# A differential-attention layer on Trainium2: context scores computed between the two maps' latent scores, with one bias operation per map

## The chip, the core and the metric

The kernel runs on one core of a Trainium2 chip. The metric is the device time of one execution in microseconds (us); a lower time is better. The core has a matrix engine (TensorE, PE in the profile; its weight loads are listed apart as PEld), a vector engine (VectorE, DVE), a scalar engine (ScalarE, ACT), GpSimd (POOL) and SyncE (SP), which issues DMAs here. Each engine runs its own queue of instructions in order, and waits on semaphores for the others.

## The reference

Four transformer layers over 1024 latent and 256 context tokens, width 1024. Layers 0 and 3 use grouped attention, layer 1 a windowed attention, layer 2 the differential attention that this change is about:

```
def diff_attention(q, k, v, lam):
    def block(j, qb):
        logits = jnp.einsum("bqhmd,bkhmd->bhmqk", qb, k).astype(jnp.float32) * scale
        p = jax.nn.softmax(logits, axis=-1)
        a = (p[:, :, 0] - lam * p[:, :, 1]).astype(v.dtype)
        return jnp.einsum("bhqk,bkhd->bqhd", a, v)
...
o = finish(diff_attention(q, jnp.concatenate([kc, k], axis=1),
                          jnp.concatenate([vc, v], axis=1), lam), s)
```

A head has two maps, m = 0 and 1, each with a softmax of its own over 256 context keys and 1024 latent keys. The second map is subtracted with the factor lam. The softmax needs the largest logit of a row, as a bias of the exponential: bias = -scale * max(largest context logit, largest latent logit).

## The kernel before

The differential layer first projects all tokens (`run_blocks`), and then attends (`project_attend`, `tile_events`, `head_c`). There are 8 heads. A head is cut into 8 tiles of 128 queries, followed by one tile for the context queries. The parts of a tile are functions: `near` (context scores of both maps and their maxima), `scores0` and `scores1` (latent scores of a map, their maximum, and the bias), `exps0` and `exps1` (the exponentials), `sums` (the factor of the second map and the combination), `turn0`, `turn_near` and `turn1` (transposes of the combined map), `products` (times v), and, every four tiles, `gate`, `scale` and `finish`.

`tile_events` gives tile number t the time t + offset for each part, with the offsets of a small table in `layer_c`, sorts all the parts by that time, and emits them so. Each of the four compute engines then keeps that order. So parts of several tiles interleave: while tile t does its scores, `sums` and `turn0` belong to tiles before it, and `turn_near`, `turn1` and `products` to the tile three before it. Loads of the next head are emitted 7 tiles ahead.

In the order before, a tile starts on TensorE with `near` (L1454: four products of 256 columns, tile `sc`), then `scores0` (L1464 by way of L1398 and L1399: four of 512 columns, tile `st`), the transposes of `turn_near` and `turn1` (tile `pT`), `scores1`, `turn0`, and `products` (tile `o`). VectorE has, for the same tile, L1456 (maximum of `sc`, two columns: one for each map), L1457 (times -scale, in place, both columns), L1466 (maximum of `st`, one column), L1467 (times -scale and the smaller of it and column m of `mx`), then L1466 and L1467 again for the second map. ScalarE's first exponential (L1478 for the context, L1482 for the latent keys) reads column m of `mx`. GpSimd combines the maps after L1405 of `sums`: L1412 and L1413 on the context part (`pc`), then on the upper half of the latent part (`p`); VectorE does the lower half in L1492.

PSUM has two tag groups: `pa`, two buffers of 1024 columns (the `st` tiles), and `pb`, four buffers of 512 columns (`sc`, all `pT`, `o`). A tile of a group takes the buffer that was released longest ago, and its first product waits until the last reader of that buffer is done.

Of the kernel before, what the change touches and what calls it, by code (L numbers as in the profile page):

```python
# [15 lines left out]
ALU = mybir.AluOpType  # L16
# [4 lines left out]
P = 128  # L21
# [51 lines left out]
class Net:  # L73
# [1285 lines left out]
    def head_c(self, q, k, i0, vsrc, gain, og, pair, need_ctx):  # L1359


        nc = self.nc
        SC = HD**-0.5
# [27 lines left out]
        def group(g, nq):  # L1391
            st["s", g] = self.small([P, 4, 2], "cs", 6)
            st["ss", g] = self.small([P, 16], "ss", 6)[:, :nq]
            st["o", g] = self.slot([P, 4, P], name="ol")[:, :nq]

        def product(ps, q_, key, m, sl):
            k1, k2 = st[key, m][1:]
            nc.tensor.matmul(ps, q_, k1[:, sl], start=True, stop=False)  # L1398
            nc.tensor.matmul(ps, q_[0 : HD + 1], k2[0 : HD + 1, sl], start=False, stop=True)  # L1399
# [43 lines left out]
        def tile(j):  # L1443
            t = self.Tile()
            g, i = j // 4, j % 4
            d = {}

            def near():

                if i == 0:  # L1450
                    group(g, 4)
                pc = d["pc"] = self.pb("sc").rearrange("p (m k) -> p m k", m=2)
                for m in range(2):
                    product(pc[:, m, :], st["lat", m][0][:, j * P : (j + 1) * P], "ctx", m, slice(0, CTX))  # L1454
                mx = d["mx"] = self.small([P, 2], "mx", 4)
                nc.vector.tensor_reduce(out=mx, in_=pc, axis=AX.X, op=ALU.max)  # L1456
                nc.vector.tensor_scalar_mul(mx, mx, -SC)  # L1457

            def scores(m):
                mx = d["mx"]  # L1460
                ps = d["ps", m] = self.pa("st")
                for c in range(2):
                    sl = slice(c * 512, c * 512 + 512)
                    product(ps[:, sl], st["lat", m][0][:, j * P : (j + 1) * P], "lat", m, sl)  # L1464
                ml = self.small([P, 1], "ml", 4)
                nc.vector.tensor_reduce(out=ml, in_=ps, axis=AX.X, op=ALU.max)  # L1466
                nc.vector.scalar_tensor_tensor(  # L1467
                    out=mx[:, m : m + 1], in0=ml, scalar=-SC, in1=mx[:, m : m + 1], op0=ALU.mult, op1=ALU.min
                )

            def exps(m):
                mx, pc = d["mx"], d["pc"]
                if m == 0:
                    d["s"] = self.small([P, 2, 2], "sm", 4)
                    both = self.slot([P, 3, CTX], name="pc")
                    d["xc"], d["tc"] = both[:, :2], both[:, 2]
                s = d["s"]
                nc.scalar.activation(  # L1478
                    d["xc"][:, m, :], pc[:, m, :], AF.Exp, scale=SC, bias=mx[:, m : m + 1], accum_out=s[:, m, 0:1]
                )  # L1480
                x = d["x", m] = self.slot([P, SEQ], name="p")
                nc.scalar.activation(  # L1482
                    x, d["ps", m], AF.Exp, scale=SC, bias=mx[:, m : m + 1], accum_out=s[:, m, 1:2]
                )

            def sums():
                s, xc = d["s"], d["xc"]
                x0, x1 = d["x", 0], d["x", 1]
                S = st["s", g][:, i : i + 1, :]
                nc.vector.tensor_tensor(S[:, 0], s[:, :, 0], s[:, :, 1], op=ALU.add)  # L1490
                r = ratio(S)
                nc.vector.scalar_tensor_tensor(  # L1492
                    out=x0[:, :512], in0=x1[:, :512], scalar=r, in1=x0[:, :512], op0=ALU.mult, op1=ALU.add
                )
                combine(xc[:, 0, :], xc[:, 1, :], r)
                combine(x0[:, 512:], x1[:, 512:], r)

            def turn(h):
                if h == 0:
                    d["t"] = self.slot([P, SEQ], name="pt")  # L1500
                pt = self.pb("pT")
                for b in range(4):
                    sl = slice((h * 4 + b) * P, (h * 4 + b + 1) * P)
                    nc.tensor.transpose(pt[:, b * P : (b + 1) * P], d["x", 0][:, sl], self.ident)
                half = d["t"][:, h * 512 : h * 512 + 512]
                if h:
                    nc.scalar.activation(half, pt, AF.Copy)
                else:
                    nc.vector.tensor_copy(half, pt)

            def turn_near():
                pt = self.pb("pT")
                for b in range(2):
                    sl = slice(b * P, (b + 1) * P)
                    nc.tensor.transpose(pt[:, sl], d["xc"][:, 0, sl], self.ident)
                nc.scalar.activation(d["tc"], pt[:, :CTX], AF.Copy)

            def products():
                cut = lambda a, b: a[:, b * P : (b + 1) * P]
                value(g, i, [(cut(d["tc"], b), 8 + b) for b in range(2)] + [(cut(d["t"], b), b) for b in range(8)])  # L1520

            if i == 3:
                last(t, g, 4)
            t.near, t.sums, t.products, t.turn_near = near, sums, products, turn_near
            t.scores0, t.scores1 = lambda: scores(0), lambda: scores(1)
            t.exps0, t.exps1 = lambda: exps(0), lambda: exps(1)
            t.turn0, t.turn1 = lambda: turn(0), lambda: turn(1)
            return t
# [47 lines left out]
    def layer_c(self, l, j, need_ctx, extra):  # L1576
        ins, nc = self.ins, self.nc
        w = ins["c_w_in"][j]
        init = 0.8 - 0.6 * math.exp(-0.3 * l)
        pairs = 5 if need_ctx else 4  # L1580
        sg = self.small([P, 1], "subg", 1)
        g = ins["c_subln_g"]
        self.queue(lambda: self.dma(sg, bass.AP(tensor=g.tensor, offset=g.offset + j * P, ap=[[1, P], [1, 1]])))
        self.in_order(lambda: nc.vector.tensor_scalar_mul(sg, sg, 1.0 - init), self.order)

        kscr = [self.Heads(self, "k", swap=True) for _ in range(2)]
        qscr = [self.Heads(self, "q") for _ in range(2)]
        vscr = [self.dram([TOK, 512], name="v") for _ in range(2)]
        ktab = self.rope_tables(ins["c_k_g"][j : j + 1])
        qtab = self.rope_tables(ins["c_q_g"][j : j + 1])  # L1590
        whole = lambda f, n: self.pair_steps([(slice(0, 512), f)], n)
        blocks = [(1024 + b * 512, whole(self.proj_qk(kscr[b], *ktab), 5)) for b in range(2)]
        blocks += [(b * 512, whole(self.proj_qk(qscr[b], *qtab), pairs)) for b in range(2)]
        blocks += [(2048 + b * 512, whole(self.proj_rows(vscr[b]), 5)) for b in range(2)]
        groups = range(3 if need_ctx else 2)
        blocks += [(3072 + b * 512, self.z_steps(4 * b, groups)) for b in range(2)]
        self.in_order(lambda: setattr(self, "lam", self.lambdas(j, init)), self.order)
        og = self.og
        vc, heads = {}, []

        def vget(b):
            if b not in vc:
                vc[b] = []
                for t0, n in GROUPS:
                    s = self.slot([P, n, 256], name="vl")
                    cs = slice(b % 2 * 256, b % 2 * 256 + 256)
                    self.dma(s, vscr[b // 2][t0 * P : (t0 + n) * P, cs].rearrange("(t p) c -> p t c", p=P))
                    vc[b].append(s)
            return vc[b]

        for b in range(4):
            for pr in range(2):

                def vsrc(b=b, pr=pr):
                    vt = vget(b)
                    return lambda kt: vt[kt // 4][:, kt % 4, pr * P : (pr + 1) * P]

                heads.append(
                    self.head_c(
                        qscr[b // 2], kscr[b // 2], b % 2 * 4 + 2 * pr, vsrc, sg, og, 2 * b + pr, need_ctx  # L1620
                    )
                )
        offsets = dict(
            near=0, scores0=0.01, scores1=0.13, exps0=0.21, exps1=0.22, sums=1.58, turn0=2.6, turn_near=3.04,
            turn1=3.08, products=3.82, gate=4.09, scale=5.77, finish=6.75,
        )
        self.project_attend(w, blocks, self.tile_events(heads, offsets, extra), 0)
        return og
# [105 lines left out]
```

## Time and profile before

| what | value |
|---|---|
| median of 3 runs | 3613.51 us (3613.27 to 3614.67) |
| the profiled execution's own time | 3609.91 us |
| its span, first to last instruction | 3608.1 us |
| PE busy | 3471.8 us (96% of the span) |
| DVE busy | 2057.5 us (57%) |
| POOL busy | 1915.1 us (53%) |
| ACT busy | 1320.9 us (37%) |
| DMA, mean share of 16 engines | 34.5% |

Shares over the whole span average over four different layers. The attention of the differential layer is the stretch from about 2267 to 2704 us, 437 us or 12% of the span. A busy PE is not PE at its peak, since matmuls overlap and their ends are modelled. "Idle before" is time in which an engine had nothing running, with the instruction that released it. A row of an instruction gives its duration from start to end; on VectorE the next instruction can start a little before the one ahead has ended.

### The profile page before, as it was taken

The page shows a single profiled execution, that of the slowest core. Times are in us where ns is not written, and L with a number is a line of the kernel's source. Part 1 is how long each engine was busy: PE and PEld are TensorE (multiplying, and loading weights), DVE is VectorE, ACT ScalarE, POOL GpSimd, SP SyncE. Part 2 cuts the span into 40 slices and gives each one's busy share as a digit, 9 for nine tenths or more (in the row PEclk, how much of TensorE's full clock was granted, in tenths as well). Part 3 has the DMA queues.
Part 4 walks back from the last instruction along what each step waited for, and adds up shares of the span by engine and source line. Part 5 has one row for each costly group of instructions (what it writes and reads, how often), then busy time and mean ns, then how long its engine had stood idle before and what let it go on. Part 6 is the DMA issues. An engine that isn't in the chain of part 4 may idle for free.

```text
span 3608.1 us, 49956 instructions
## 1 busy us (share of the span) xinstructions
PE 3471.8 (96%) x18594; PEld 2608.3 (72%) x18594; DVE 2057.5 (57%) x3358; ACT 1320.9 (37%) x2756; POOL 1915.1 (53%) x1854
## 2 busy tenths in 40 slices
PE   7999999998999999999999999999999999999989
PEld 4887444446788888887878888888887787554447
DVE  5552555665641412888566610799994654466653
ACT  3221444451321212774222211677771322344430
POOL 5540666677531311667565510566775643377884
PEclk9999999999999999999999999999999999999999
DMA  6343443513344434552425531221312335111113
GB/s 211 78 122 101 140 138 113 192 56 97 122 105 129 111 123 113 169 153 69 146 79 140 136 114 56 84 82 44 96 42 95 120 79 142 47 40 44 45 41 88
DMA packets 229453, 370.33 MB, mean 103 GB/s; under 512 B 34088, under 2 KB 124120, under 8 KB 229212
## 3 DMA queue, kind: packets, MB, share of 16 engines
q1 hardware_dynamic: 228636, 367.01, 34.5%
q8 instruction: 147, 2.41, 0.3%
q14 instruction: 94, 0.77, 0.1%
q10 hardware_dynamic: 576, 0.15, 0.0%
HBM read 270.36 MB, written 96.57 MB: 102 GB/s over the span
## 4 chain that ended last, share of the span: by engine, by line
PE 73%; DVE 14%; POOL 7%; issue 3%; ACT 1%; DMA 1%; SPq 0%; POOLq 0%; ACTq 0%; DVEq 0%
PE proj L382 22%; PE zT L467 11%; PE y L911 9%; PE o L739 7%; PE st L714 4%; PE st L715 4%; DVE ml L1466 3%; PE sl L670 2%; PE o L1136 2%; POOL p L753 2%; DVE wlo L133 1%; PE qkT L437 1%; POOL rstd L146 1%; PE ada L195 1%; PE pT L1214 1%
## 5 line engine op out<-in xcount | busy, mean ns | idle before, releaser
L753 POOL TENSOR_TENSOR p<-p,p 128x1024 f32<-128x1024 f32 x224 | 540.1, 2411 | 303.6 <-PE o L739 258.2
L382 PE MATMUL proj<-whi,hhi 128*128 128x512 f32 x1408 | 556.3, 395 | 3.7 <-POOL whi L130 2.4
L382 PE MATMUL proj<-wlo,hhi 128*128 128x512 f32 x1408 | 550.8, 391 | 3.0 <-DVE wlo L133 3.0
L382 PE MATMUL proj<-whi,hlo 128*128 128x512 f32 x1408 | 550.4, 391 | 0.0
L719 ACT ACTIVATE p<-st 128x1024 f32<-128x1024 f32 (+1 forms) x336 | 324.1, 1003 | 286.2 <-PE st L715 274.3
L911 PE MATMUL y<-whi,ogt 128*128 128x512 f32 x1216 | 387.5, 396 | 13.2 <-POOL ogt L130 9.4
L661 DVE TENSOR_REDUCE M<-sl 128x1 f32<-128x512 f32 (+1 forms) x326 | 209.8, 685 | 293.2 <-PE sl L670 243.5
L133 DVE TENSOR_TENSOR wlo<-wraw,whi 128x1024 fp32r<-128x1024 f32 x136 | 217.3, 1612 | 221.6 <-POOL whi L130 196.3
L739 PE MATMUL o<-p,v 128*64 128x512 f32 x1344 | 321.2, 599 | 0.0
L130 POOL TENSOR_SCALAR whi<-wraw 128x1024 fp32r<-128x1024 f32 x136 | 178.7, 1319 | 252.6 <-DMA wraw<-in_c_w_in_dram 86.0
L382 PEld LDWEIGHTS proj<-whi,hhi 128*128 128x128 f32 x1408 | 265.7, 189 | 57.9 <-POOL whi L130 2.6
L382 PEld LDWEIGHTS proj<-wlo,hhi 128*128 128x128 f32 x1408 | 265.6, 189 | 57.6 <-DVE wlo L133 4.7
L382 PEld LDWEIGHTS proj<-whi,hlo 128*128 128x128 f32 x1408 | 265.3, 188 | 55.2
L911 PEld LDWEIGHTS y<-whi,ogt 128*128 128x128 f32 x1216 | 229.8, 189 | 67.8 <-POOL ogt L130 11.6
L467 PE MATMUL zT<-hhi,whi 128*128 128x512 f32 (+1 forms) x704 | 256.9, 365 | 5.6 <-DVE qklo L133 5.6
L404 ACT ACTIVATE y<-proj 128x1024 f32<-128x1024 f32 (+1 forms) x68 | 65.6, 964 | 527.0 <-PE proj L382 469.4
L467 PE MATMUL zT<-hhi,wlo 128*128 128x512 f32 (+1 forms) x704 | 254.5, 362 | 1.3 <-DVE wlo L133 1.3
L467 PE MATMUL zT<-hlo,whi 128*128 128x512 f32 (+1 forms) x704 | 254.5, 362 | 0.0
L911 PE MATMUL y<-wlo,ogt 128*128 128x512 f32 x608 | 238.6, 392 | 0.0
L146 POOL TENSOR_TENSOR rstd<-rstd,mhalf 128x16 f32<-128x16 f32 (+3 forms) x132 | 231.0, 1750 | 10.9
L714 PE MATMUL st<-q,k 128*128 128x512 f32 x512 | 217.8, 425 | 10.5 <-DVE M L658 7.2
L658 DVE TENSOR_REDUCE M<-sl 128x2 f32<-128x1024 f32 (+1 forms) x165 | 200.6, 1216 | 45.2 <-PE sl L670 40.1
(221 smaller groups left out, 7035.2 us busy)
## 6 DMA issues: line engine op xcount, KB each, us to landing
adaw<-in_ada_w_dram SPq DMA_DIRECT2D x96, 512.0 KB
xo<-xres SPq DMA_DIRECT2D x86, 256.0 KB
wraw<-in_a_w_in_dram SPq DMA_DIRECT2D x40, 512.0 KB
k<-k SPq DMA_DIRECT2D x40, 512.0 KB
q<-qkhi SPq DMA_DIRECT2D x76, 256.0 KB
q<-qklo SPq DMA_DIRECT2D x76, 256.0 KB
q<-q SPq DMA_DIRECT2D x136, 128.0 KB
wraw<-in_b_w_in_dram SPq DMA_DIRECT2D x32, 512.0 KB
```

Of the source, the lines that this page charges most:

```text
L130: self.nc.gpsimd.tensor_scalar(out=out, in0=in_, scalar1=1.0, scalar2=0.0, op0=ALU.mult, op1=ALU.add)
L133: self.nc.vector.tensor_tensor(out, a, b, op=ALU.subtract)
L146: nc.gpsimd.tensor_tensor(r, r, self.mhalf[:, :n], op=ALU.pow)
L382: nc.tensor.matmul(ps[:, i, :], self.h_op(a, 2 * tp + i, k), wop(b, k), start=(k == 0 and j == 0), stop=(k == KT - 1 and j == 2),)
L467: nc.tensor.matmul(ps, wop(a, k)[:, b * P : (b + 1) * P], self.h_cols(c, g, k), start=(k == 0 and j == 0), stop=(k == KT - 1 and j == 2),)
L658: nc.vector.tensor_reduce(out=out, in_=both.rearrange("p (h q k) -> p h q k", h=2, q=n), axis=AX.X, op=ALU.max)
L661: nc.vector.tensor_reduce(out=out[:, hh, :], in_=ps[hh].rearrange("p (q k) -> p q k", q=n), axis=AX.X, op=ALU.max)
L714: nc.tensor.matmul(ps[:, hh, :], self.k_op(K, 0, kt), q1[:, hh, :], start=True, stop=False)
L719: nc.scalar.activation(p, ps, AF.Exp, scale=HD**-0.5)
L739: nc.tensor.matmul(st["o"][hh * HD : (hh + 1) * HD, :], v(hh, kt), p[:, hh, :], start=j == 0, stop=j == N - 1, tile_position=(0, hh * HD),)
L753: eng.tensor_tensor(a, a, p, op=ALU.add)
L911: nc.tensor.matmul(ps, ot[a][:, k, :], wop[h](b, k), start=(k == 0 and j == 0), stop=(k == KT - 1 and j == 2))
```

## The change

The score of map 0 over the latent keys now comes first, the context scores second (between `turn_near` and `turn1` of the tile three before), and the score of map 1 third, where it was. The scaling of both context maxima (L1457) is gone. In its place a map's bias is made by one operation: the larger of its two maxima, times -scale. It is a `tensor_scalar` that takes the latent maximum as its tensor and the context maximum as a per-partition scalar read from SBUF; before it was a `scalar_tensor_tensor` with two tensors.

```
+            def bias(m):
+                mx = d["mx"][:, m : m + 1]
+                nc.vector.tensor_scalar(out=mx, in0=d["ml", m], scalar1=mx, scalar2=-SC, op0=ALU.max, op1=ALU.mult)
...
                 nc.vector.tensor_reduce(out=mx, in_=pc, axis=AX.X, op=ALU.max)
-                nc.vector.tensor_scalar_mul(mx, mx, -SC)
+                bias(0)
...
-                ml = self.small([P, 1], "ml", 4)
+                ml = d["ml", m] = self.small([P, 1], "ml", 4)
                 nc.vector.tensor_reduce(out=ml, in_=ps, axis=AX.X, op=ALU.max)
-                nc.vector.scalar_tensor_tensor(
-                    out=mx[:, m : m + 1], in0=ml, scalar=-SC, in1=mx[:, m : m + 1], op0=ALU.mult, op1=ALU.min
-                )
+                if m:
+                    bias(m)
...
-            near=0, scores0=0.01, scores1=0.13, exps0=0.21, exps1=0.22, sums=1.58, turn0=2.6, turn_near=3.04,
+            scores0=0, near=0.07, scores1=0.13, exps0=0.21, exps1=0.22, sums=1.58, turn0=2.6, turn_near=3.04,
```

On VectorE, in one tile in the middle of the first head, these rows stood between two L1492 before (`sc`, `st` and `pT` are PSUM tiles, `mx` and `ml` the maxima):

```order
L1492 SCALAR_TENSOR_TENSOR p_19207<-p_19210,rs_19285,p_19207 128x512
L1509 COPY pt_19293<-pT_19294 128x512
L1421 COPY ol_18951<-o_19300 128x128
L1456 TENSOR_REDUCE mx_19319<-sc_19314 128x2
L1457 TENSOR_SCALAR mx_19319<-mx_19319 128x2
L1466 TENSOR_REDUCE ml_19327<-st_19322 128x1
L1467 SCALAR_TENSOR_TENSOR mx_19319<-ml_19327,mx_19319 128x1
L1466 TENSOR_REDUCE ml_19345<-st_19340 128x1
L1467 SCALAR_TENSOR_TENSOR mx_19319<-ml_19345,mx_19319 128x1
```

The same tile in the changed kernel (its line numbers are 1 to 3 higher; L1450 is the new operation, L1469 the latent maximum, L1460 the context maximum):

```order
L1494 SCALAR_TENSOR_TENSOR p_19202<-p_19205,rs_19279,p_19202 128x512
L1511 COPY pt_19287<-pT_19288 128x512
L1421 COPY ol_18958<-o_19294 128x128
L1469 TENSOR_REDUCE ml_19313<-st_19308 128x1
L1460 TENSOR_REDUCE mx_19324<-sc_19319 128x2
L1450 TENSOR_SCALAR mx_19324<-ml_19313,mx_19324 128x1
L1469 TENSOR_REDUCE ml_19338<-st_19333 128x1
L1450 TENSOR_SCALAR mx_19324<-ml_19338,mx_19324 128x1
```

One operation of the six is gone, the two first maxima have changed places, and the bias of map 0 stands behind both of them.

On TensorE the start of a tile of the second head before was this:

```order
L1398 MATMUL sc_19607<-kc_19047,q_3440_19034 128x256
L1399 MATMUL sc_19607<-kc_19047,q_3440_19034 128x256
L1398 MATMUL sc_19607<-kc_19047,q_3443_19041 128x256
L1399 MATMUL sc_19607<-kc_19047,q_3443_19041 128x256
L1398 MATMUL st_19615<-k_3439_19033,q_3440_19034 128x512
L1399 MATMUL st_19615<-k_3441_19035,q_3440_19034 128x512
L1398 MATMUL st_19615<-k_3439_19033,q_3440_19034 128x512
L1399 MATMUL st_19615<-k_3441_19035,q_3440_19034 128x512
L1515 MATMUL pT_19623<-ident,pc_19427 128x128 x2
L1504 MATMUL pT_19627<-ident,p_19429 128x128 x4
```

And this is the same place in the changed kernel:

```order
L1398 MATMUL st_19598<-k_3439_19030,q_3440_19031 128x512
L1399 MATMUL st_19598<-k_3441_19032,q_3440_19031 128x512
L1398 MATMUL st_19598<-k_3439_19030,q_3440_19031 128x512
L1399 MATMUL st_19598<-k_3441_19032,q_3440_19031 128x512
L1517 MATMUL pT_19605<-ident,pc_19419 128x128 x2
L1398 MATMUL sc_19609<-kc_19044,q_3440_19031 128x256
L1399 MATMUL sc_19609<-kc_19044,q_3440_19031 128x256
L1398 MATMUL sc_19609<-kc_19044,q_3443_19038 128x256
L1399 MATMUL sc_19609<-kc_19044,q_3443_19038 128x256
L1506 MATMUL pT_19617<-ident,p_19421 128x128 x4
```

The four context products have moved behind the first latent score and two transposes of an older tile; they now stand between two groups of transposes. The count of products is the same, and the rows of ScalarE, GpSimd and SyncE come in the same order as before.

## Rows read from the trace of the kernel before

**Rows 1.** Windows: stretch, us, PE, PEld, DVE, ACT, POOL busy, clock, DMA, GB/s.

```profile
2267.00:2704.00 437.00, 407.68 (x2836) 367.43 (x2835) 407.81 (x826) 323.24 (x919) 298.08 (x412) 0.96 0.22 66
...
2426.31:2481.09 54.78, 51.47 (x369) 46.89 (x368) 51.28 (x106) 41.26 (x120) 38.32 (x55) 0.97 0.25 79
...
2446.15:2449.82 3.67, 3.67 (x15) 3.18 (x15) 3.08 (x7) 2.23 (x7) 3.17 (x8) 0.54 0.00 0
```

**Rows 2.** Waits, 2267 to 2704 us: who for whom, total us, times, longest.

```profile
PE sc L1398 <- ACT pc L1478: 21.7, 15, 2.2
...
DVE ml L1466 <- PE st L1399: 8.7, 14, 1.8
```

**Rows 3.** Timeline of a steady tile, VectorE, then GpSimd: start, duration.

```profile
2301.62 0.75 DVE L1492 SCALAR_TENSOR_TENSOR p<-p,rs,p 128x512 f32<-128x512 f32 x1
...
2303.08 0.68 DVE L1456 TENSOR_REDUCE mx<-sc 128x2 f32<-128x512 f32 x1
2303.80 0.43 DVE L1457 TENSOR_SCALAR mx<-mx 128x2 f32<-128x2 f32 x1
2304.13 1.21 DVE L1466 TENSOR_REDUCE ml<-st 128x1 f32<-128x1024 f32 x1
2305.38 0.20 DVE L1467 SCALAR_TENSOR_TENSOR mx<-ml,mx 128x1 f32<-128x1 f32 x1
2305.50 1.21 DVE L1466 TENSOR_REDUCE ml<-st 128x1 f32<-128x1024 f32 x1
...
2307.47 0.75 DVE L1492 SCALAR_TENSOR_TENSOR p<-p,rs,p 128x512 f32<-128x512 f32 x1
...
2303.51 0.70 POOL L1412 TENSOR_SCALAR p<-p,rs 128x512 f32<-128x512 f32 x1
2304.29 1.27 POOL L1413 TENSOR_TENSOR p<-p,p 128x512 f32<-128x512 f32 x1
```

**Rows 4.** Groups by form, 2267 to 2704 us: busy us, mean ns | idle before.

```profile
L1478 ACT ACTIVATE pc<-sc,mx 128x256 f32<-128x256 f32 x128 | 60.6, 473 | 71.5 <-DVE mx L1467 71.0 <-DMA vl<-v 0.6
...
L1457 DVE TENSOR_SCALAR mx<-mx 128x2 f32<-128x2 f32 x64 | 31.0, 484 | 2.2
L1467 DVE SCALAR_TENSOR_TENSOR mx<-ml,mx 128x1 f32<-128x1 f32 x128 | 27.4, 214 | 4.4
```

**Rows 5.** Timeline, the second tile behind a context tile: GpSimd, VectorE, TensorE.

```profile
2442.58 1.27 POOL L1413 TENSOR_TENSOR p<-p,p 128x512 f32<-128x512 f32 x1
...
2443.01 0.85 DVE L1467 SCALAR_TENSOR_TENSOR mx<-ml,mx 128x1 f32<-128x1 f32 x1
...
2446.15 0.39 PE L1398 MATMUL sc<-kc,q 128*128 128x256 f32 x1 [2.16 <-ACT pc L1478]
```

**Rows 6.** Lines of VectorE: count, shortest, median and longest ns.

```profile
L1457 DVE TENSOR_SCALAR mx<-mx x64: 168/431/1229, 2269.0 to 2698.4; 128x2 f32<-128x2 f32 x64
...
L1356 DVE TENSOR_SCALAR lam<-lam x1: 148/148/148, 1834.8 to 1834.8; 128x1 f32<-128x1 f32 x1
...
L1405 DVE SCALAR_TENSOR_TENSOR rs<-rs,lam,cs x72: 219/219/457, 2278.0 to 2710.0; 128x1 f32<-128x1 f32 x64, 128x2 f32<-128x2 f32 x8
...
L305 DVE TENSOR_SCALAR hs<-xT,colA,colS x160: 390/402/413, 33.4 to 2866.2; 128x128 f32<-128x128 f32 x160
```

**Rows 7.** Timeline: a one-column reciprocal while a GpSimd operation runs.

```profile
2645.18 0.16 DVE L1404 RECIPROCAL rs<-cs 128x1 f32<-128x1 f32 x1
...
2645.04 0.69 POOL L1412 TENSOR_SCALAR p<-p,rs 128x512 f32<-128x512 f32 x1
```

**Rows 8.** Timeline of TensorE over one tile, from its first product to the next's.

```profile
2466.61 0.39 PE L1398 MATMUL sc<-kc,q 128*128 128x256 f32 x1 [0.89 <-ACT pc L1478]
2466.83 0.28 PE L1399 MATMUL sc<-kc,q 65*128 65x256 f32 x1
2466.95 0.28 PE L1398 MATMUL sc<-kc,q 128*128 128x256 f32 x1
...
2472.32 0.36 PE L1398 MATMUL sc<-kc,q 128*128 128x256 f32 x1
```

More of the change, by code (lines that the diff above doesn't have):

```diff
@@ L1456, in near @@
                 nc.vector.tensor_reduce(out=mx, in_=pc, axis=AX.X, op=ALU.max)
-                nc.vector.tensor_scalar_mul(mx, mx, -SC)
+                bias(0)
             def scores(m):
-                mx = d["mx"]
                 ps = d["ps", m] = self.pa("st")
```

## The prediction

> **What bounds the stage now.** I cut the span into windows first, since the change touches one stage alone: the attention of the differential layer, 437 us long [rows 1]. There PE is busy for 407.7 us and DVE for 407.8, so each leaves about 29 us, and neither is plainly the bound. The waits by engine come next: PE waits 21.7 us, in 15 waits, for ScalarE's context exponential before its `sc` products, and DVE waits only 8.7 us for PE's scores [rows 2]. So DVE has next to no waits: its remaining idle time is the small gap in front of an operation that reads the result of the one ahead. Then I read a steady tile on DVE, from one L1492 to the next: 2307.47 - 2301.62 = 5.85 us without a pause [rows 3]. PE needs 2472.32 - 2466.61 = 5.71 us for a tile in which it doesn't wait [rows 8]. The stage runs at DVE's pace, with PE 0.14 us per tile behind it, which matters below.
>
> The rows of that tile show where DVE loses time. L1457, a product over two columns, takes 0.43 us and ends at 2304.23, when GpSimd's L1412 ends (2303.51 + 0.70 = 2304.21). L1467 ends at 2305.58, with GpSimd's L1413 (2305.56) [rows 3]. Over 64 executions L1457's shortest is 0.168 us and its longest 1.229 [rows 6]. In the second tile behind a context tile L1467 takes 0.85 us and ends at 2443.86, again with GpSimd's addition at 2443.85 [rows 5]. So these small DVE operations on SBUF are held until GpSimd's operation is over, and a DVE queue without slack passes the hold on to everything.
>
> **The change, part by part.**
> L1457 leaves. Its mean is 0.484 us in 64 executions [rows 4]; in the steady tile 0.43 + 2303.80 - 2304.13 = 0.10 us of it lie under the next row [rows 3]. DVE's queue gets 64 x 0.384 = 24.6 us back.
>
> The two maxima change places. L1466 and L1467 start 1.25 us apart, since one reads the other [rows 3]. An independent successor would start 1.21 - 0.10 = 1.11 us behind; I take 1.13, between that and the end. So 0.12 x 64 = 7.7 us come back.
>
> The new operation replaces L1467, mean 0.214 [rows 4]. No row has this form, a one-column `tensor_scalar` with a scalar read from SBUF. Lower bound: 0.148 us, a one-column `tensor_scalar` with constants (L1356). Upper bound without a hold: L1405, one column with an SBUF scalar, 0.219 [rows 6]. I take 0.22, as the scalar is read in both: 128 x (0.220 - 0.214) = 0.8 us lost. With a hold it costs up to L1457's 1.229, when it meets GpSimd's longest operation; that is the first rival. DVE in all: 24.6 + 7.7 - 0.8 = 31.5 us, or 0.49 us per tile.
>
> PE pays for the new order. The first of the `sc` products after products of another kind takes 2466.83 - 2466.61 = 0.22 us to the next, the second 0.12 [rows 8]: 0.10 us for such a switch. Before, a tile has two switches to score products (at `sc` and at the second `st`); now it has three (first `st`, `sc`, second `st`). 64 x 0.10 = 6.4 us. So PE needs 5.81 us for a steady tile, and DVE, with no hold, about 5.85 - 0.33 - 0.12 - 0.04 + 0.12 = 5.48: the 0.33 is L1457's place up to the next start, the 0.12 the swap, the 0.04 L1467's hold (0.20 less the 0.16 that is left without one), the second 0.12 the scalar read in two operations. **PE becomes the bound of the steady tiles, and they gain 0.04 us, not 0.37.** The gain must come from tiles in which PE waits now.
>
> Those are two per head. In the second tile behind a context tile PE waits 2.16 us [rows 5]. `sc` of the next tile there takes the buffer of the present `sc`, so it waits for the second map's context exponential, and that stands behind the held L1467. Without the hold the bias of map 0 is ready about 1.0 us earlier: L1467's 0.85 - 0.16 = 0.69 us of hold and L1457's place, 0.38 us on the mean, go; the scalar read takes 0.06 back. Besides, the next tile now starts on PE with `st`, which waits for the first map's exponential, one context exponential (0.47 us, [rows 4]) sooner. The wait shrinks by some 1.45 to about 0.7 us. The other wait is 0.89 us [rows 8]; in the tile ahead of it L1457 sits under a whole 1.2 us addition, and I take 0.85 off. That is 2.3 us per head, 18.4 us over eight heads, of the 21.7. Behind the long wait the granted clock is 0.54 of full for 3.67 us [rows 1], which costs 3.67 x 0.46 = 1.7 us; six heads show the mean clock of 0.97 of the one in [rows 1], so 10 us in all. If the clock stays up with a 0.7 us pause, all of it comes back, if not, none; I take half, 5 us. Of PE's other idle time, 29.3 - 21.7 = 7.6 us, I take a third, 2.5.
>
> Sum: 18.4 + 5 + 2.5 - 6.4 = 19.5 us. The bounds without a hold: PE never idle and at full clock gives 29.3 + 10 - 6.4 = 33, and DVE's 31.5 caps it there; two thirds of the waits, no clock, and the switches in full give 12.3 - 6.4 = 6.
>
> The profiled execution took 3609.91 us (span 3608.1); 3609.9 - 19.5 = 3590.4. The median of the runs is 3.6 us above that execution, so the forecast for the median is 3594.
>
> **Will the new operation be held?** L1467 reads two tensors from SBUF, and it is held. L1457 reads one with two columns, and it is held. What the new one shares with the ones that are not: the reciprocal L1404, one tensor and one column, runs in 0.16 us at 2645.18 in the middle of GpSimd's L1412 (2645.04 to 2645.73) [rows 7]; L305 reads two scalars from SBUF beside a PSUM tensor and stays within 0.390 to 0.413 us in 160 executions [rows 6]. So neither one column nor a scalar is held by itself. And L1457's floor over two columns is 0.168, 0.020 above L1356's one column [rows 6], more than one more column should cost if both ran alike. All three are indirect. [...]
>
> **Rivals.**
> *Held after all* (chance 0.24). In the steady tile the new L1450 would start at 1.46 (L1456's present place) + 1.13 + 0.72 (L1456 to its reader) = 3.31 us behind L1492, at 2304.93, under the addition that ends at 2305.56; the second maximum would start at 2305.50, exactly as now [rows 3]. So the steady tile stays at 5.85. The second tile behind a context tile stays held up to 2443.86, and only the 0.47 us of the earlier exponential remain; the 0.85 us of the other wait may still go, since the operation moves there behind the addition. (0.47 + 0.85) x 8 = 10.6, less 6.4 for PE: 4 us faster, 3609 to 3610 for the median, between 3605 and 3614.
>
> *A buffer wait that takes the place of the hold* (chance 0.08; slower). With the new order `sc` takes, in most tiles, the buffer that the `sc` of the tile before has just left, so its first product waits for the second context exponential of that tile; before, a transposition behind eight score products had that wait. For it: this is the kind of wait that costs 21.7 us now. Against it: four `st` products and two transposes, about a microsecond of work, now run ahead of it. PE's slack per tile is (54.78 - 51.47 = 3.31 us idle in a head [rows 1] + 1.7 of clock) / 8 = 0.63, less 0.10 for the switch. It decides from 0.53 us per tile on; at 0.8 the stage loses 64 x 0.27 = 17 us, and the median would be 3631.
>
> *Not held, as forecast* (0.66), with its own range of 3582 to 3607. The remaining 0.02 I leave to no change.
>
> **Chances and range.** About 0.2% (7 us) is what a measurement of this kernel can tell from no change. Not held: faster 0.63, same 0.03. Held: faster 0.06, same 0.16, slower 0.02. The buffer wait: slower 0.08. With the 0.02 of no change that is 0.69 faster, 0.21 same, 0.10 slower. The range takes in the first case and most of the second: 3581 to 3612.
>
> **What the profile after would show.** Right: L1450 near 0.22 us in all 128 executions, also under GpSimd's additions; steady tiles of about 5.8 us, with PE without pause and DVE waiting for `st`; PE's wait behind the context tiles well under 2.16 us; the granted clock no longer at 0.54 there. The switch shows as a third product row of 0.2 us or more to the next in each tile. Wrong: L1450 with a median above 0.4 us and ends that coincide with GpSimd's; or PE waits for the context exponential in most tiles. The sum is wrong with the mechanism right if the clock still falls behind the shorter wait, or if `st` at a tile's start waits for the first map's exponential in steady tiles.

## The result: 3591.2 us, and the profile after

The changed kernel takes 3591.24 us, the median of four runs (3590.24 to 3592.09), beside 3613.98 for the kernel before (3613.27 to 3614.67). The ratio is 0.9939 with a 95% interval of 0.9926 to 0.9951: faster by 22.7 us. The forecast was 3594.0.

The stage first, as one window: from the first score product to the first product of the output projection (L911). First the kernel before, whose rows ahead of the prediction were cut at other times; then the changed kernel, with one head. Columns as in [rows 1].

```profile
2267.60:2727.50 459.90, 423.10 (x2929) 380.32 (x2928) 422.58 (x852) 333.11 (x954) 317.66 (x443) 0.95 0.22 65
```

```profile
2271.50:2709.97 438.47, 413.68 (x2929) 373.11 (x2928) 397.19 (x788) 332.89 (x954) 316.09 (x443) 0.97 0.22 68
...
2425.18:2476.89 51.71, 50.00 (x368) 45.52 (x367) 48.22 (x97) 41.17 (x119) 37.90 (x55) 1.00 0.26 82
```

The stage is 21.4 us shorter, so nearly the whole difference lies in it. PE's idle time in it (length less busy) falls from 36.8 to 24.8 us. DVE has 25.4 us less work and 41 us of room, where it had 37. A head takes 51.7 us instead of 54.8, and its mean clock is 1.00 instead of 0.97. The chain of work that ended last says the same for the whole span: PE 78% and DVE 9%, where it was PE 73% and DVE 14%.

Does the new operation wait for GpSimd? The line of VectorE, with count and shortest, median and longest ns, of the changed kernel:

```profile
L1450 DVE TENSOR_SCALAR mx<-ml,mx x128: 212/214/216, 2274.5 to 2684.0; 128x1 f32<-128x1 f32 x128
```

It does not, in any of 128 executions; L1457, which it made superfluous, went up to 1229 ns [rows 6]. By the two engines' timelines, 32 of the 128 ran wholly inside an L1412 or L1413 of GpSimd, with 0.05 us or more left at both ends; of the 192 L1457 and L1467 before, none did. The steady tile on VectorE and the last GpSimd row beside it:

```profile
2301.48 0.75 DVE L1494 SCALAR_TENSOR_TENSOR p<-p,rs,p 128x512 f32<-128x512 f32 x1
...
2303.07 1.23 DVE L1469 TENSOR_REDUCE ml<-st 128x1 f32<-128x1024 f32 x1
2304.21 0.68 DVE L1460 TENSOR_REDUCE mx<-sc 128x2 f32<-128x512 f32 x1
2304.93 0.21 DVE L1450 TENSOR_SCALAR mx<-ml,mx 128x1 f32<-128x1 f32 x1
2305.15 1.22 DVE L1469 TENSOR_REDUCE ml<-st 128x1 f32<-128x1024 f32 x1
2306.41 0.21 DVE L1450 TENSOR_SCALAR mx<-ml,mx 128x1 f32<-128x1 f32 x1
2306.54 0.15 DVE L1492 TENSOR_TENSOR cs<-sm 128x2 f32<-128x2 f32 x1
...
2307.18 0.75 DVE L1494 SCALAR_TENSOR_TENSOR p<-p,rs,p 128x512 f32<-128x512 f32 x1
```

```profile
2304.15 1.28 POOL L1413 TENSOR_TENSOR p<-p,p 128x512 f32<-128x512 f32 x1
```

L1450 runs at 2304.93 in the middle of the addition (2304.15 to 2305.43) and takes its 0.21 us. The tile is 2307.18 - 2301.48 = 5.70 us long, where it was 5.85 [rows 3].

PE's waits in the stage, and the second tile behind a context tile, which answers to [rows 5]:

```profile
PE st L1398 <- ACT p L1484: 13.1, 11, 2.5
PE pT L1564 <- POOL p L1413: 2.6, 2, 1.4
PE oT L1436 <- ACT ol L1430: 2.3, 2, 1.6
PE pT L1506 <- DVE pt L1511: 2.1, 4, 0.7
...
PE sc L1398 <- DVE pt L1511: 1.3, 8, 0.2
```

```profile
2443.69 0.50 PE L1398 MATMUL st<-k,q 128*128 128x512 f32 x1 [1.17 <-ACT p L1484]
...
2445.27 0.39 PE L1398 MATMUL sc<-kc,q 128*128 128x256 f32 x1 [0.16 <-DVE pt L1511]
```

The 21.7 us of waits for the context exponential [rows 2] are gone. A wait of `st` for the first map's exponential, 13.1 us, stands in their place. Behind a context tile it is 1.17 us instead of 2.16. The other wait of a head, 0.89 us [rows 8], has no successor in its place; in three heads a wait of 0.38 to 0.73 us for VectorE's copy (L1511) is new.

### The profile page after: what moved, and what is told of

The parts are those of the page before. It is cut to its first block, busy times and chain, and to the rows that moved or that the text cites. A ratio compares the mean times of both kernels' runs of the same rounds, so it can differ in the third digit from the quotient of the medians.

```text
span 3590.1 us, 49903 instructions
## 1 busy us (share of the span) xinstructions
PE 3466.3 (97%) x18594; PEld 2601.9 (72%) x18594; DVE 2030.3 (57%) x3294; ACT 1320.0 (37%) x2756; POOL 1913.2 (53%) x1854
## 4 chain that ended last, share of the span: by engine, by line
PE 78%; DVE 9%; POOL 7%; issue 3%; DMA 2%; ACT 1%; SPq 0%; ACTq 0%; POOLq 0%; DVEq 0%
PE proj L382 22%; PE zT L467 11%; PE y L911 9%; PE o L739 7%; PE st L714 4%; PE st L715 4%; PE o L1418 3%; PE sl L670 2%; POOL p L753 2%; PE o L1136 2%; DVE wlo L133 2%; PE qkT L437 1%; DVE ml L1469 1%; PE st L1398 1%; PE st L1399 1%
## 5 line engine op out<-in xcount | busy, mean ns | idle before, releaser
L911 PE MATMUL y<-whi,ogt 128*128 128x512 f32 x1216 | 387.6, 396 | 13.0 <-POOL ogt L130 9.4
L911 PEld LDWEIGHTS y<-whi,ogt 128*128 128x128 f32 x1216 | 230.0, 190 | 67.8 <-POOL ogt L130 12.4
L911 PE MATMUL y<-wlo,ogt 128*128 128x512 f32 x608 | 238.7, 393 | 0.0
```

The costliest lines, as they stand in the source:

```text
L911: nc.tensor.matmul(ps, ot[a][:, k, :], wop[h](b, k), start=(k == 0 and j == 0), stop=(k == KT - 1 and j == 2))
```

## The experiments

Theory A says that the gain comes from the form of the bias operations, which GpSimd no longer holds. Theory B puts it down to the new order. Theory C puts it down to VectorE's smaller number of operations. D and E ask which engine sets the pace afterwards, TensorE (D) or still VectorE (E). The table gives for each run its median, its ratio to the kernel before on the same chip, and from its trace the length of the stage, the clock loss in it (in windows of 1 us, one less the granted clock, summed) and the difference of the two. The last column takes out the clock loss, which varied from one trace to another. It takes out too much: of the changed kernel's middle heads (the second to the seventh, cut where VectorE starts on the maxima of the context queries' tile) one has a clock loss of 1.7 us and is only 0.5 to 0.8 us longer than the others, as the last section shows; so a run with a larger loss looks better in this column than it is.

| run | median us | ratio (95%) | stage us | clock loss | rest |
|---|---|---|---|---|---|
| before | 3613.98 | 1 | 459.9 | 22.8 | 437.1 |
| changed | 3591.24 | 0.9939 (0.9926 to 0.9951) | 438.5 | 14.0 | 424.5 |
| form only | 3591.61 | 0.9943 (0.9929 to 0.9956) | 436.5 | 11.3 | 425.2 |
| order only | 3611.37 | 0.9999 (0.9990 to 1.0007) | 459.2 | 20.6 | 438.6 |
| held form | 3604.51 | 0.9976 (0.9965 to 0.9986) | 449.2 | 15.4 | 433.8 |
| more operations, none held | 3599.31 | 0.9957 (0.9944 to 0.9969) | 445.2 | 17.1 | 428.1 |
| one spare | 3593.11 | 0.9950 (0.9938 to 0.9962) | 443.5 | 19.9 | 423.6 |
| three spare | 3599.14 | 0.9964 (0.9952 to 0.9976) | 446.0 | 13.9 | 432.1 |
| latent first | 3594.86 | 0.9950 (0.9938 to 0.9962) | 440.0 | 16.5 | 423.5 |
| latent first, old order | 3608.73 | 0.9988 (0.9980 to 0.9997) | 455.8 | 24.2 | 431.6 |
| latent first, map 0 | 3592.49 | 0.9940 (0.9926 to 0.9954) | 434.6 | 8.9 | 425.7 |
| changed, beside it | 3592.57 | 0.9947 (0.9935 to 0.9960) | 439.1 | 14.3 | 424.8 |

**The form alone, in the old order.** Against the changed kernel:

```
                 nc.vector.tensor_reduce(out=mx, in_=pc, axis=AX.X, op=ALU.max)
-                bias(0)
...
                 nc.vector.tensor_reduce(out=ml, in_=ps, axis=AX.X, op=ALU.max)
-                if m:
-                    bias(m)
+                bias(m)
...
-            scores0=0, near=0.07, scores1=0.13, exps0=0.21, exps1=0.22, sums=1.58, turn0=2.6, turn_near=3.04,
+            near=0, scores0=0.01, scores1=0.13, exps0=0.21, exps1=0.22, sums=1.58, turn0=2.6, turn_near=3.04,
```

> The order of before is kept (context scores first, then both latent scores), but each bias is the new one-operation form, 2 per tile, and the two-column product is gone. Theory A (the gain is that the bias operations are no longer held by GpSimd): all 128 executions near 0.22 us and a time of 3592 to 3600 us, a little above the changed kernel because the wait for the second context exponential behind the context tile stays at about 1.2 us instead of 2.16. Theory B (the gain comes from the order, latent score first): 3608 to 3616, as before. Theory C (the gain is the one operation fewer per tile on VectorE): 3590 to 3597, as the changed kernel.

It took 3591.61 us, a ratio of 0.9943. This is the whole gain without the new order. Its bias line:

```profile
L1450 DVE TENSOR_SCALAR mx<-ml,mx x128: 212/214/216, 2274.9 to 2682.4; 128x1 f32<-128x1 f32 x128
```

and on PE the second tile behind a context tile:

```profile
2439.97 0.39 PE L1398 MATMUL sc<-kc,q 128*128 128x256 f32 x1 [1.52 <-ACT pc L1478]
```

Without the hold the wait is 1.52 us. The new order takes it to 1.17, but PE's idle time in the stage is 24.8 us with it and 25.6 without, so other waits use up most of that. B falls. C is not told apart from A by this run, as the count fell too.

**The order alone, with the old operations.** Against the changed kernel:

```
-                nc.vector.tensor_scalar(out=mx, in0=d["ml", m], scalar1=mx, scalar2=-SC, op0=ALU.max, op1=ALU.mult)
+                nc.vector.scalar_tensor_tensor(
+                    out=mx, in0=d["ml", m], scalar=-SC, in1=mx, op0=ALU.mult, op1=ALU.min
+                )
...
                 nc.vector.tensor_reduce(out=mx, in_=pc, axis=AX.X, op=ALU.max)
+                nc.vector.tensor_scalar_mul(mx, mx, -SC)
                 bias(0)
```

> The new order (latent score of the first map, context scores, latent score of the second) with the three old operations: the product over two columns, and for each map the operation on two SBUF tensors. Theory A: the two-column product and the two-tensor operations are held by GpSimd in many tiles (longest over 0.8 us), VectorE keeps its old pace of about 5.85 us per tile, and the time is 3604 to 3616 us. Theory B: the first map's score starts one exponential earlier and the maxima are spread, so 3588 to 3598, as the changed kernel. Theory C: as before, 3610 to 3616.

3611.37 us, a ratio of 0.9999: the order brings nothing. VectorE, two starts of L1497 in steady tiles and the two-column product between them:

```profile
2302.86 0.75 DVE L1497 SCALAR_TENSOR_TENSOR p<-p,rs,p 128x512 f32<-128x512 f32 x1
...
2306.17 0.66 DVE L1463 TENSOR_SCALAR mx<-mx 128x2 f32<-128x2 f32 x1
2306.86 0.16 DVE L1450 SCALAR_TENSOR_TENSOR mx<-ml,mx 128x1 f32<-128x1 f32 x1
...
2308.91 0.75 DVE L1497 SCALAR_TENSOR_TENSOR p<-p,rs,p 128x512 f32<-128x512 f32 x1
```

```profile
2305.52 1.28 POOL L1413 TENSOR_TENSOR p<-p,p 128x512 f32<-128x512 f32 x1
```

The product is now held up to the end of the addition (2306.17 + 0.66 = 2306.83, and 2305.52 + 1.28 = 2306.80), and the steady tile is 6.05 us long, longer than before. PE's idle time in the stage falls from 36.8 to 32.5 us, but its busy time grows by nearly as much, from 423.1 to 426.7; where that arises was not followed.

**The same place and count, in a held form.** Against the changed kernel:

```
-                nc.vector.tensor_scalar(out=mx, in0=d["ml", m], scalar1=mx, scalar2=-SC, op0=ALU.max, op1=ALU.mult)
+                nc.vector.scalar_tensor_tensor(
+                    out=mx, in0=d["ml", m], scalar=mx, in1=self.nsc, op0=ALU.max, op1=ALU.mult
+                )
...
+        self.nsc = c([P, 1], "nsc")
+        nc.vector.memset(self.nsc, -(HD**-0.5))
```

> The changed kernel, with the same number of operations in the same places and the same result, but the bias is written as an operation on two SBUF tensors: the factor comes from a column of constants instead of from the instruction. Theory A: this form is held until GpSimd's operation ends, as the old two-tensor operation was; its mean goes from 0.214 to 0.35 us or more, with a longest above 0.6, and the time rises to 3600 to 3614 us. Theories B and C: order and count are those of the changed kernel, so the time stays within 4 us of it, 3588 to 3595.

3604.51 us. With order and count unchanged, 0.9939 (0.9947 in the changed kernel's second series) becomes 0.9976: the hold alone takes back 0.29 to 0.37%, some 10 to 13 of the 22.7 us. The group of the operation (busy us, mean ns):

```profile
L1452 DVE SCALAR_TENSOR_TENSOR mx<-ml,mx,nsc 128x1 f32<-128x1 f32 x128 | 45.1, 353 | 4.6
```

and its line:

```profile
L1452 DVE SCALAR_TENSOR_TENSOR mx<-ml,mx,nsc x128: 218/220/957, 2273.2 to 2693.8; 128x1 f32<-128x1 f32 x128
```

In a steady tile the first map's operation takes 0.65 us, up to the end of GpSimd's addition, and the second map's, behind it, 0.22:

```profile
2302.86 0.65 DVE L1452 SCALAR_TENSOR_TENSOR mx<-ml,mx,nsc 128x1 f32<-128x1 f32 x1
```

```profile
2302.22 1.27 POOL L1415 TENSOR_TENSOR p<-p,p 128x512 f32<-128x512 f32 x1
```

So the median is that of an operation that isn't held, and the mean, 353 ns against the 214 of the changed kernel's form in the same place, shows the hold. C, as the cause of the whole gain, falls with this run.

**More operations than before, none in a held form.** Against the kernel before:

```
-                nc.vector.tensor_scalar_mul(mx, mx, -SC)
+                for m in range(2):
+                    nc.vector.tensor_scalar_mul(mx[:, m : m + 1], mx[:, m : m + 1], -SC)
...
-                nc.vector.scalar_tensor_tensor(
-                    out=mx[:, m : m + 1], in0=ml, scalar=-SC, in1=mx[:, m : m + 1], op0=ALU.mult, op1=ALU.min
-                )
+                mx = mx[:, m : m + 1]
+                nc.vector.tensor_scalar(out=mx, in0=ml, scalar1=-SC, scalar2=mx, op0=ALU.mult, op1=ALU.min)
```

> The order of before, with one operation more per tile on VectorE than before and two more than in the changed kernel, none in a form that was held: two one-column products in place of the two-column one, and a one-column tensor_scalar with a constant and a scalar from SBUF in place of each two-tensor operation. Theory A: no hold, so VectorE needs 64 x (2 x 0.15 - 0.484) = 11.8 us less than before although it has more operations, and the time is 3596 to 3608 us. Theory B: no change, 3611 to 3617. Theory C: slower than before by the extra operation, 64 x 0.15 = 9.6 us, 3618 to 3626.

3599.31 us: 64 operations more than before and 0.43% faster. The two new lines:

```profile
L1458 DVE TENSOR_SCALAR mx<-mx x128: 142/149/155, 2272.0 to 2687.0; 128x1 f32<-128x1 f32 x128
L1469 DVE TENSOR_SCALAR mx<-ml,mx x128: 212/214/216, 2273.5 to 2689.7; 128x1 f32<-128x1 f32 x128
```

Two columns in one product cost 168 to 1229 ns [rows 6], two products of one column never more than 155 each. More operations and still most of the gain: that is A. But the count isn't free. Against the form-only run, which has the same order, no hold and two operations fewer per tile, this run takes 7.7 us more, and a middle head at full clock (1.00 throughout) 52.9 us instead of 51.7 to 51.8. By that, the one operation fewer of the change is worth some 4 of the 22.7 us (an estimate).

**One and three spare operations on VectorE.** Against the changed kernel, behind `bias(m)` of the second map (the count is 1 or 3):

```
+                    sp = self.small([P, 4], "spare", 2)
+                    for n in range(3):
+                        nc.vector.tensor_scalar_mul(sp[:, n : n + 1], ml, -SC)
```

> The changed kernel with one spare one-column product per tile on VectorE behind the second bias (0.15 us, its result is not read): 64 x 0.15 = 9.6 us more on VectorE. Theory D (TensorE sets the pace of the changed kernel's steady tiles and VectorE is some 0.2 us per tile ahead): no change beyond 3 us, 3589 to 3594. Rival E (VectorE still sets the pace): all 9.6 us come through, 3599 to 3603.

> The same with three spare products per tile, 64 x 0.45 = 28.6 us more on VectorE. Theory D: the slack of 0.2 us per tile is used up and the rest comes through, 64 x 0.25 = 16 us, so 3602 to 3611. Rival E: all of it, 3617 to 3623. If VectorE were free by more than 0.45 us per tile: 3589 to 3594.

One spare: 3593.11 us, near the changed kernel's 3591.24 and 3592.57. Three: 3599.14, with a stage 7.5 us longer, less than the 16 that D gave. The expectation had the wrong price. The three products of a steady tile:

```profile
2305.64 0.21 DVE L1450 TENSOR_SCALAR mx<-ml,mx 128x1 f32<-128x1 f32 x1
2305.78 0.26 DVE L1474 TENSOR_SCALAR spare<-ml 128x1 f32<-128x1 f32 x3
2305.96 0.15 DVE L1495 TENSOR_TENSOR cs<-sm 128x2 f32<-128x2 f32 x1
```

The three, of which none reads another and each takes 142 to 147 ns, start 0.06 us apart ((0.26 - 0.14) / 2). From L1450 to the sums it takes 0.32 us here and 0.13 in the changed kernel, so three cost 0.19 us per tile, 12 us in all, not 28.6; and one costs 0.06, under 4 us in all, which can't be told from nothing by these medians. The steady tiles of the first head don't lengthen (5.65 us with three, 5.70 without): there D holds.

In the heads behind it, D doesn't hold. One middle head at full clock with one spare operation per tile, then one with three, in the columns of [rows 1]:

```profile
2476.67:2528.80 52.13, 50.48 (x368) 45.57 (x367) 48.95 (x107) 41.29 (x120) 37.85 (x55) 1.00 0.24 70
```

```profile
2479.11:2531.91 52.80, 50.36 (x368) 45.45 (x367) 49.80 (x122) 41.32 (x119) 37.90 (x55) 1.00 0.26 69
```

Of the middle heads, those at full clock take 51.7 to 52.0 us in the changed kernel, 51.9 to 52.1 with one spare, 52.8 to 52.9 with three. Of the 8 x 0.19 = 1.5 us that three spares add to a head's eight tiles, about 1.0 comes through. So VectorE still sets the pace of a part of these heads, and its rows agree: in the changed kernel's head from 2580.13 to 2632.03 us it waits longer than 0.11 us only twice, both times for a latent score:

```profile
2590.45 1.23 DVE L1469 TENSOR_REDUCE ml<-st 128x1 f32<-128x1024 f32 x1 [0.64 <-PE st L1399]
...
2596.14 1.22 DVE L1469 TENSOR_REDUCE ml<-st 128x1 f32<-128x1024 f32 x1 [0.50 <-PE st L1399]
```

**The latent exponential first.** The remaining 1.17 us behind a context tile looked like the chain of maxima, bias and two exponentials. Exchanging the two `activation` calls in `exps` puts the one that frees the score buffer first. It was run on the changed kernel, on the form-only kernel, and on the changed kernel for the first map alone. The exchange:

```
+                x = d["x", m] = self.slot([P, SEQ], name="p")
+                nc.scalar.activation(
+                    x, d["ps", m], AF.Exp, scale=SC, bias=mx[:, m : m + 1], accum_out=s[:, m, 1:2]
+                )
                 nc.scalar.activation(
                     d["xc"][:, m, :], pc[:, m, :], AF.Exp, scale=SC, bias=mx[:, m : m + 1], accum_out=s[:, m, 0:1]
                 )
-                x = d["x", m] = self.slot([P, SEQ], name="p")
-                nc.scalar.activation(
-                    x, d["ps", m], AF.Exp, scale=SC, bias=mx[:, m : m + 1], accum_out=s[:, m, 1:2]
-                )
```

> The changed kernel with the two exponentials of each map in the other order on ScalarE: the latent one (1.10 us), which frees the score buffer for which the next tile's first product waits, ahead of the context one (0.47 + 0.20 us). If the 1.17 us wait behind each context tile is the chain of the two maxima, the bias and these two exponentials, it falls to about 0.5 us: 7 x 0.67 us, and 1 to 2 us in the first head, 5 to 6 us faster than the changed kernel, 3583 to 3588. If something else decides that wait, 3589 to 3594.

> The order of before with the one-operation bias (as in the form-only run), and the two exponentials of each map exchanged as in the run beside it. There the next tile begins with the context scores, which wait for the second map's context exponential; that now stands behind a 1.10 us exponential more. If this chain decides the wait of 1.52 us behind each context tile, it grows to about 2.6 us: 7 x 1.1 = 8 us slower than the form-only run, 3597 to 3604, and more where the clock falls behind the longer wait. If not, 3590 to 3594.

> The changed kernel with the exchange for the first map alone: ScalarE runs the first map's latent exponential, its context exponential, then the second map's context and latent ones. The first latent exponential, which frees the score buffer, comes 0.67 us earlier; the second context exponential stays where it was. If the 0.91 us wait of the near transposition in the run with both exchanged came from the second map's context exponential standing behind a latent one, that wait doesn't appear here and 1.17 us falls to 0.71: 7 x 0.46 = 3.2 us and about 1 us in the first head, 3585 to 3589, or 3 to 5 us under the changed kernel beside it. If that wait came from something else, it stays and the time is that of the changed kernel within 2 us.

The first brought nothing (3594.86 us). The second was slower than the form-only kernel by more than expected, 0.9988 against 0.9943: its wait is 2.65 us, as expected, and adds to a rest that is 6.4 us longer, but the clock loss grew by another 12.9. The third equals the changed kernel that ran beside it.

> The changed kernel itself, on the chip of the run beside it, as its base: 3590 to 3594 us; and a second trace, in which the part of the program ahead of the attention should end 3 to 5 us later than in the profiled execution of the kernel before, as in all traces since, if that one was an early outlier.

PE behind a context tile, with both maps exchanged:

```profile
2440.96 0.50 PE L1398 MATMUL st<-k,q 128*128 128x512 f32 x1 [0.71 <-ACT p L1481]
...
2443.09 0.41 PE L1517 MATMUL pT<-ident,pc 128*128 128x128 f32 x2 [0.91 <-POOL rstd L144]
```

and with the first map alone, PE and then VectorE's copy:

```profile
2441.12 0.50 PE L1398 MATMUL st<-k,q 128*128 128x512 f32 x1 [0.71 <-ACT p L1488]
...
2443.16 0.39 PE L1398 MATMUL sc<-kc,q 128*128 128x256 f32 x1 [0.61 <-DVE pt L1517]
```

```profile
2442.43 0.68 DVE L1517 COPY pt<-pT 128x512 f32<-128x512 f32 x1
```

The wait falls to 0.71 us as expected, and another takes its place a microsecond later: `sc` waits for a buffer until VectorE's copy is over at 2443.11. 0.71 + 0.61 = 1.32 us, where the changed kernel has 1.17 + 0.16 = 1.33. By these rows VectorE's queue still sets the pace behind a context tile, and ScalarE's order only moves the wait. That the 0.91 us wait was the second context exponential's buffer is likely, since it is gone in the third run; it wasn't tried otherwise. No version beat the changed kernel.

## Why the prediction was right

**Whether the new operation is held.** It isn't: 212 to 216 ns, 0.22 forecast. The three indirect signs held good, the weakest of them too: between L1456 and L1466 a column more costs (1.21 - 0.68) / 512 us, 1.0 ns (an estimate from [rows 3]), not the 20 ns of that sign, and one column against two decided the product's hold in the fourth experiment. There 256 executions of two forms with one column show none, at 142 to 155 and 212 to 216 ns, where L1457 with its two took up to 1229 [rows 6].

**VectorE's term.** L1457's 31.0 us left the stage, and 25.4 of them are gone from VectorE's busy time. Nearly all the rest came back as holds of the operations behind: the sums' two-tensor additions (L1490 before, L1492 after) went from a mean of 153 to 215 ns (the longest from 156 to 1242) and L1405 from 223 to 243, (0.062 + 0.020) x 64 = 5.2 us. The prediction hadn't seen that a hold avoided by one operation may meet the next. What that cost in time wasn't tried.

**PE as the new bound.** Right for the steady tiles of the first head, which gained 0.15 us, not 0.04, and didn't lengthen with spare operations. Not right for the heads behind it, which are most of the stage. There a head lost 54.78 - 51.71 = 3.07 us, the clock's part included, and VectorE 51.28 - 48.22 = 3.06 us of busy time in it; and about two thirds of three spare operations came through. The prediction took VectorE's freed time as a cap alone and looked for the gain in TensorE's waits; the two are accounts of the same time, and the spare runs show that VectorE's queue still counts. **The switch's 6.4 us were mis-sized: they are nil.** A tile in which PE doesn't wait, in the changed kernel:

```profile
2432.88 0.47 PE L1398 MATMUL st<-k,q 128*128 128x512 f32 x1
2433.20 0.39 PE L1399 MATMUL st<-k,q 65*128 65x512 f32 x1
...
2433.89 0.38 PE L1517 MATMUL pT<-ident,pc 128*128 128x128 f32 x2
2434.03 0.36 PE L1398 MATMUL sc<-kc,q 128*128 128x256 f32 x1
2434.23 0.28 PE L1399 MATMUL sc<-kc,q 65*128 65x256 f32 x1
...
2438.56 0.48 PE L1398 MATMUL st<-k,q 128*128 128x512 f32 x1
```

The two transposes in the kernel before, and what followed them:

```profile
2468.14 0.38 PE L1515 MATMUL pT<-ident,pc 128*128 128x128 f32 x2
2468.36 0.60 PE L1504 MATMUL pT<-ident,p 128*128 128x128 f32 x4
```

The third switch is there: 0.32 us at `st`, 0.20 at `sc`. But the two transposes take 0.14 us to the next start, where they took 0.22 ahead of other transposes before, and the tile takes 5.68 us against 5.71 [rows 8]. PE's busy time less the clock loss was 423.1 - 22.8 = 400.3 us, and is 413.7 - 14.0 = 399.7.

**The waits.** 18.4 and 2.5 us were forecast; PE's idle time fell by 12.0. The wait behind a context tile shrank to 1.17 us, not 0.7. By the form-only run the missing hold is worth 2.16 - 1.52 = 0.64 us of it, not 1.0, and the order 0.35, not 0.47. The prediction also counted eight heads where seven have such a tile ahead of them, and the first head's waits for the first map's exponential grew from 1.85 + 0.70 + 0.99 to 2.49 + 1.36 + 0.50 us. The other wait of a head went as forecast.

**The clock.** 5 us were forecast, between 0 and 10; the clock loss fell by 8.8. In PE's account the measured terms are 12.0 + 8.8 + 0.6 = 21.4 us, and the forecast was 18.4 + 5 + 2.5 - 6.4 = 19.5. The gain from the waits was put 8.9 us too high, that from the switch 7.0 and that from the clock 3.8 too low. That the sum came within 2 us is luck. Nor are the terms separate causes: the fall of the clock in the changed kernel lengthened its head by 0.5 to 0.8 us with a clock loss of 1.7, as the last section shows.

**The order.** Right in what it does to each row, but the prediction gave it 7.7 us on VectorE and a part of the waits. The order-only run shows it worth nothing with the holds in place, and the form-only run worth nothing without them.

**The 3.6 us** between the profiled execution and the median most likely lay ahead of the stage, whose first score product started at 2267.60 us, and between 2270.2 and 2272.6 in all eleven later traces, of which the order-only one has a stage as long as before and ran in 3611.37. The rival's wait of `sc` for the context exponential didn't appear; what `sc` waits for is VectorE's copy, 1.3 us in eight waits.

## What to carry to other kernels

When VectorE's small operations end together with GpSimd's, look at their form before their number: here one tensor in SBUF with one column, and the second value as a per-partition scalar, wasn't held (212 to 216 ns), while two columns (up to 1229 ns) or two tensors (up to 957) were. A queue freed so can hand the pace to another engine in some tiles and keep it in others; a few spare operations put into it tell where, once their price is read from the trace (three left a steady tile here at 5.65 us and made a middle head 52.8 to 52.9 us long instead of 51.7 to 52.0). A wait that is shortened by reordering one engine can be worth nothing while another queue ends just behind it, as 0.71 + 0.61 us against 1.17 + 0.16 showed: sum the waits over a few microseconds, not at one row.

## What the runs showed of the hardware

The clock's answer to a wait was not decided by its length alone. The granted clock fell for part of the 3.6 us behind all six waits of 1.89 to 2.16 us in the middle heads before, to a mean of 0.53 to 0.68 of full there; behind the wait of [rows 5] it stood at 0.50 from 2446.5 to 2449.75 us. It fell behind one of seven waits of 1.16 to 1.17 us in the changed kernel (0.79), two of seven of 1.50 to 1.52 us in the form-only run (0.73 and 0.83), and two of six of 1.50 to 1.63 us in the held-form run (0.80 and 0.72), where the three longest passed without a fall. The two windows of the changed kernel:

```profile
2443.69:2447.29 3.60, 3.44 (x19) 2.75 (x20) 3.56 (x7) 3.06 (x10) 3.10 (x9) 1.00 0.00 0
2495.50:2499.10 3.60, 3.44 (x16) 2.89 (x17) 3.56 (x7) 2.85 (x10) 3.18 (x8) 0.79 0.00 0
```

Both stand behind a wait of 1.17 us; what sets them apart stays open. In the changed kernel's second trace the fall stands behind the same one of the seven, the fourth, with 0.76 in its 3.6 us, so it may not be chance.

A fall cost less than it seems. The head of the changed kernel with that fall:

```profile
2475.63:2528.12 52.49, 51.17 (x368) 46.84 (x367) 47.67 (x98) 41.75 (x120) 38.14 (x55) 0.97 0.24 70
```

The clock loss in it is 1.7 us, but it is only 0.5 to 0.8 us longer than the other middle heads (51.7 to 52.0 us), since PE waits less: 52.49 - 51.17 = 1.3 us idle, where the head shown with the result has 1.7. In the other runs that have middle heads with and without a fall, those with one are 0.1 to 1.4 us longer in the mean. So the 8.8 us of clock loss that went are worth less than 8.8 us of the stage's 21.4, and runs of this stage are best compared by heads at full clock.
